# Sparse attention in a two-layer trunk: small reciprocals, and weight remainders by an accumulating DMA

## The chip, the cores and the metric
One core of a Trainium2 chip runs the whole program. The metric is device microseconds of one execution. TensorE multiplies matrices, VectorE and ScalarE do elementwise work, GpSimd (POOL in the profile) does elementwise work in SBUF and issues DMAs, SyncE (SP) issues DMAs.

## What is computed
The trunk has two layers on 512 tokens of width 1024. Layer 0 mixes tokens by a gated linear recurrence (HGRN), layer 1 by sparse attention; each is followed by a feed-forward block with a convolution. The change touches layer 1 alone:

```python
def dsa_mixer(x, w_in, w_out, rel_bias):        # shortened
    q, k, v, q_idx, k_idx, w_idx = jnp.split(x @ w_in, cuts, axis=-1)
    # 16 query heads and 2 key heads of 64, 8 index heads of 64
    dots = jnp.einsum('bthd,bsd->bths', qib, k_idx)
    scores = jnp.einsum('bths,bth->bts', jax.nn.relu(dots), wb)
    scores = jnp.where(admissible, scores, NEG_BIG)
    _, sel = lax.top_k(scores, top_k)           # top_k = 128
    logits = einsum(q, k[sel]) * 64 ** -0.5 + rel_bias[bucket(q_pos - sel)]
    probs = jax.nn.softmax(jnp.where(valid, logits, NEG_BIG), axis=-1)
    return einsum(probs, v[sel]) @ w_out
```

## The kernel before
Every f32 matrix product is made of three products in a reduced format: each operand is split into a large part and the remainder, and `mm3` adds large by large, large by remainder and remainder by large. `wunit` loads one unit of weights (up to 128x1024) into `wr` and splits it: ScalarE copies the large part `whi`, another engine subtracts it from the raw weights and writes the remainder `wlo`. Each of the tags `wr`, `whi` and `wlo` has three buffers. The list `lo_engine` says who makes the remainder: VectorE, GpSimd, or, where it holds `None`, no engine. In that last form ScalarE writes the negated large part into `wlo`, and a DMA issued by GpSimd reads the raw weights from DRAM once more and adds them to it. The HGRN layer's second half uses that form (19 units); the sparse attention doesn't.

A projection of 128 columns (`proj_T`) is eight calls of `mm3`, 24 matmuls, for one unit of weights. In the sparse attention there are fifteen: the index key and index weights (72 columns), four blocks of index queries, K, V, and eight blocks of queries, in that order (`head_in`, then `rest_in`). The remainders of the first two units are made by VectorE, those of the next eleven by GpSimd, those of the last two query blocks by VectorE.

The order on TensorE is the order in which the program emits its matmuls: a main generator is woven with side generators, by estimated TensorE times written in the code. Beside `head_in` run the norm (`norm_chain`, whose line 253 copies the reciprocal row scales on ScalarE) and `setup` (four loads of shifted bias rows from the DRAM tensor Z by SyncE, lines 728 to 734, copied into `bias` by ScalarE). Beside `rest_in` run `dots` (index scores on VectorE, line 764), `top` (sixteen rounds of finding and striking out the eight largest, lines 778 and 780, then a mask, line 783) and `attend`. On all the other engines a planner orders the instructions at build time, by emission order and by the costs and ready times that it reckons with; at run time each engine keeps that order.

`attend` goes through 16 units of half the tokens and two heads each. `scores` multiplies queries and keys, adds the mask as a product with the identity (line 863) and the bias on VectorE (line 873, which also takes a minimum), and makes the exponentials with their sums on ScalarE (line 892). The reciprocals of the sums stand in `rs`, each repeated over 64 columns, since TensorE transposes them together with the probabilities (lines 914 and 917). `mixv` copies the transposed block to SBUF on ScalarE (`px`, line 918), multiplies by the values (lines 925 and 928) and scales on VectorE (line 932). `stack` writes large parts on ScalarE (lines 675 and 676) and remainders on VectorE or GpSimd (677 and 678); `scaled` evacuates a product through ScalarE and GpSimd (699 and 700). `kw_weights` transposes the index weights on TensorE (line 717) and needs the row scales.

Of the kernel before, what the change touches and what calls it, by code (L numbers as in the profile page):

```python
# [17 lines left out]
P = 128  # L18
# [30 lines left out]
def trunk(ctx: ExitStack, tc: tile.TileContext, xT, vecs, convs, hgrn_w_in, hgrn_w_out, dsa_w_in, dsa_w_out,  # L49
          rel_bias, ffn_w_up, ffn_w_down, c_masks, c_onehot, out, dbg=None, stop=99):  # L50
    nc = tc.nc
# [85 lines left out]
    lo_engine = [nc.vector]  # L137
# [49 lines left out]
    def add_side(gen, rate=1.0):  # L187
        side.append([gen, rate, 0.0])

    def step(e):  # L190
        c = next(e[0], None)
        if c is None:
            side.remove(e)
        else:
            e[2] -= c

    def weave(gen):
        for c in gen:
            for e in list(side):
                e[2] += c * e[1]  # L200
                while e in side and e[2] > 0:
                    step(e)
# [458 lines left out]
    with ExitStack() as sx:  # L661
# [26 lines left out]
        with ExitStack() as sy:  # L688
# [33 lines left out]
            def setup():  # L722

                yield 7.0
                nc.vector.tensor_copy(identb, ident)
                nc.gpsimd.memset(vf, 0.0)
                for h in range(0, AH, 4):
                    nc.scalar.activation(bias[:, h:h + 4, :256], far[:, h:h + 4, None].to_broadcast([P, 4, 256]),
                                         AF.Copy, scale=-1.0)

                    back = ix.tile([P, 4, 256], F32, name="back", bufs=2)
                    nc.sync.dma_start(back, bass.AP(tensor=Z.tensor, offset=Z.offset + h * BAND,
                                                    ap=[[1, P], [BAND, 4], [1, 256]]))
                    nc.scalar.activation(bias[:, h:h + 4, 256:], back[:, :, ::-1], AF.Copy)
                    yield 3.0

            def head_in():
                pk = yield from proj_T(w_in, O_KI, 72)
                for b in range(4):
                    o = yield from proj_T(w_in, O_QI + b * P,  # L740
                                          hook=({7: lambda: kw_evac(pk)}, {2: kw_weights}, None, None)[b])
                    lo_engine[0] = nc.gpsimd
                    stack(4 + b, o, nc.vector)

            def dots():
# [57 lines left out]
            def rest_in():  # L803
                pk = yield from proj_T(w_in, O_K)
                pv = yield from proj_T(w_in, O_V, hook={3: lambda: k_out(pk)})
                for b in range(KB):
                    lo_engine[0] = nc.vector if b >= 6 else nc.gpsimd
                    o = yield from proj_T(w_in, b * P, hook={3: lambda: kw.append(scaled(pv)), 7: v_out}
                                          if b == 0 else None)
                    tmp = scaled(o, P, -0.125)  # L810
                    stack(b, tmp, nc.gpsimd)
                    done.add(f"q{b}")
                done.add("q8")

            add_side(norm_chain())
            add_side(setup())
            weave(head_in())
            add_side(dots(), 1.0)
            rest = rest_in()
            for c in rest:  # L820
                weave([c])
# [16 lines left out]
        def scores(u):  # L838


            hf, b = u
# [45 lines left out]
            sm = at.tile([P, 2, 2], F32, name="sm", bufs=4)  # L887
            rs = at.tile([P, 2, 2, 64], F32, name="rs", bufs=4)
            for e in range(2):
                for j, t in enumerate(tiles):  # L890
                    l = L[e][j][:, :(t + 1) * P]
                    nc.scalar.activation(l, l, AF.Exp, bias=mn[e][:, j:j + 1], scale=-1.0, accum_out=sm[:, j, e:e + 1])
            nc.vector.reciprocal(rs, sm[:, :, :, None].to_broadcast([P, 2, 2, 64]))
            probs[u] = L, rs
            if {"sel3", "q8"} <= done:
                later = [c for f, c in units[units.index(u) + 1:] if f]
# [144 lines left out]
```

## Time and profile before

| | |
|---|---|
| median of 3 runs | 1279.28 us (1279.26 to 1279.95) |
| profiled execution | 1283.4 us |
| its span, first to last instruction | 1281.6 us |
| mean granted TensorE clock | 0.991 |
| TensorE busy | 1256.1 us, 98% |
| VectorE busy | 820.5 us, 64% |
| ScalarE busy | 597.3 us, 47% |
| GpSimd busy | 155.8 us, 12% |

The profile is of one execution; the runs are timed without it. Times of rows are microseconds from the span's start unless marked ns. Matmuls are pipelined, so a busy TensorE is not one at its peak. A granted clock of 1.00 is 2.4 GHz; the other level is 1.2 GHz, and a stretch between 0.5 and 1.00 had both. The sparse attention up to its output product takes the stretch from 669 to 860 us.

### The profile page before, as it was taken

What the parts mean: (1) busy time and instruction counts of PE and PEld (TensorE: products, weight loads), DVE (VectorE), ACT (ScalarE), POOL (GpSimd) and SP (SyncE); (2) the same over time, 40 slices, a digit from 0 to 9 for tenths busy, and PEclk for the clock granted to TensorE, in tenths of its full rate; (3) what the DMA queues carried; (4) which work ended last, traced back from release to release, by engine and by line L of the source; (5) the groups of instructions that cost most, each with busy time, mean ns of one, the idle gap of its engine ahead of it and who ended that gap; (6) DMA issues with size and microseconds to landing.
All of it is one profiled execution on the core that took longest, in us unless ns stands there. A gap on an engine that the chain in (4) does not pass through costs nothing.

```text
span 1281.6 us, 15660 instructions
## 1 busy us (share of the span) xinstructions
PE 1256.1 (98%) x6054; PEld 1050.0 (82%) x6054; DVE 820.5 (64%) x1279; ACT 597.3 (47%) x991; POOL 155.8 (12%) x130
## 2 busy tenths in 40 slices
PE   8999999999999999999999998999999999999997
PEld 7788888888888888888877777898888888888886
DVE  7755777756777777732434999945677777762331
ACT  5446565454544444422336657854444444441330
POOL 3023223110000000000004574210000000000000
PEclk9999999999999999999999989999999999999998
DMA  6339777223333333323244220102333333333222
GB/s 198 116 80 152 131 131 132 67 66 99 97 93 92 97 99 99 99 99 99 76 114 134 65 66 17 34 1 84 97 99 99 98 93 92 95 99 99 91 75 66
DMA packets 190857, 119.84 MB, mean 94 GB/s; under 512 B 5136, under 2 KB 180160, under 8 KB 190784
## 3 DMA queue, kind: packets, MB, share of 16 engines
q1 hardware_dynamic: 170320, 108.31, 28.5%
q0 software_dynamic: 19760, 9.96, 6.4%
q8 instruction: 47, 0.77, 0.2%
q10 hardware_dynamic: 704, 0.58, 0.2%
q14 instruction: 26, 0.21, 0.1%
HBM read 116.72 MB, written 2.12 MB: 93 GB/s over the span
## 4 chain that ended last, share of the span: by engine, by line
PE 90%; DVE 6%; ACT 1%; issue 1%; DMA 0%; POOL 0%; POOLq 0%; DVEq 0%; ACTq 0%
PE pj L169 17%; PE pj L170 17%; PE pj L171 17%; PE px L169 9%; PE px L171 9%; PE px L170 9%; PE pav L925 2%; PE pl L556 1%; PE po L602 1%; DVE scs L764 1%; PE pl L866 1%; PE pt L914 1%; PE pn L169 1%; PE pn L171 1%; PE pn L170 1%
## 5 line engine op out<-in xcount | busy, mean ns | idle before, releaser
L169 PE MATMUL pj<-x,whi 128*128 128x512 f32 (+1 forms) x1016 | 404.9, 398 | 0.0
L170 PE MATMUL pj<-x,whi 128*128 128x512 f32 (+1 forms) x1016 | 398.2, 392 | 0.0
L171 PE MATMUL pj<-x,wlo 128*128 128x512 f32 (+1 forms) x1016 | 398.1, 392 | 0.0
L143 ACT ACTIVATE whi<-wr 128x1024 fp32r<-128x1024 f32 (+1 forms) x175 | 181.9, 1040 | 253.6 <-PE px L170 152.3
L144 DVE TENSOR_TENSOR wlo<-wr,whi 128x1024 fp32r<-128x1024 f32 (+2 forms) x165 | 202.0, 1225 | 152.4 <-ACT whi L143 150.3
L171 PEld LDWEIGHTS pj<-x,wlo 128*128 128x128 f32 (+1 forms) x1016 | 191.8, 189 | 41.2
L169 PEld LDWEIGHTS pj<-x,whi 128*128 128x128 f32 (+1 forms) x1016 | 192.1, 189 | 39.6 <-issue 1.6
L170 PEld LDWEIGHTS pj<-x,whi 128*128 128x128 f32 (+1 forms) x1016 | 192.0, 189 | 38.9 <-issue 1.0
L169 PE MATMUL px<-ah,whi 128*128 128x512 f32 (+1 forms) x332 | 128.5, 387 | 0.0
L171 PE MATMUL px<-ah,wlo 128*128 128x512 f32 (+1 forms) x332 | 127.5, 384 | 0.0
L170 PE MATMUL px<-al,whi 128*128 128x512 f32 (+1 forms) x332 | 126.3, 381 | 0.0
L348 DVE TENSOR_TENSOR ub<-pj,rstd_r 128x512 f32<-128x512 f32 x88 | 60.6, 688 | 82.8 <-PE pj L171 77.9
L143 ACT ACTIVATE ah<-c 128x512 fp32r<-128x512 f32 x44 | 27.8, 631 | 115.9 <-DVE c L360 115.9
L171 PEld LDWEIGHTS px<-ah,wlo 128*128 128x128 f32 x332 | 62.3, 188 | 13.5
L170 PEld LDWEIGHTS px<-al,whi 128*128 128x128 f32 x332 | 62.4, 188 | 12.7
L351 ACT ACTIVATE c<-ub,convc 128x512 f32<-128x512 f32 x88 | 71.2, 809 | 2.4 <-DVE ub L348 1.6
L169 PEld LDWEIGHTS px<-ah,whi 128*128 128x128 f32 x332 | 62.5, 188 | 11.4
L353 DVE SCALAR_TENSOR_TENSOR c<-ub,convc,c 128x512 f32<-128x512 f32 x88 | 66.1, 752 | 3.0
L352 DVE SCALAR_TENSOR_TENSOR c<-ub,convc,c 128x512 f32<-128x512 f32 x88 | 65.6, 746 | 0.0
L358 ACT ACTIVATE c<-c 128x512 f32<-128x512 f32 x44 | 27.8, 632 | 80.5 <-DVE c L353 80.4
L522 DVE TENSOR_TENSOR qk<-qk,ftree 128x512 f32<-128x512 f32 x56 | 39.6, 709 | 18.9 <-PE pl L560 7.1
L144 DVE TENSOR_TENSOR al<-c,ah 128x512 fp32r<-128x512 f32 x44 | 30.5, 692 | 29.3 <-ACT ah L143 29.3
(226 smaller groups left out, 1768.8 us busy)
## 6 DMA issues: line engine op xcount, KB each, us to landing
wr<-in_ffn_w_up_dram SPq DMA_DIRECT2D x88, 512.0 KB, 3.8
wr<-in_ffn_w_down_dram SPq DMA_DIRECT2D x41, 512.0 KB, 3.7
wr<-in_hgrn_w_in_dram SPq DMA_DIRECT2D x30, 512.0 KB, 4.2
wlo<-in_hgrn_w_in_dram POOLq DMA_DIRECT2D x19, 512.0 KB, 7.7
wr<-in_dsa_w_in_dram SPq DMA_DIRECT2D x14, 512.0 KB, 3.7
wr<-in_hgrn_w_out_dram SPq DMA_DIRECT2D x8, 512.0 KB, 3.7
wr<-in_dsa_w_out_dram SPq DMA_DIRECT2D x8, 512.0 KB, 3.8
back<-Z SPq DMA_DIRECT2D x4, 512.0 KB, 5.1
```

Of the source, the lines that this page charges most:

```text
L143: nc.scalar.activation(dst_h, src, AF.Copy)
L144: lo.tensor_tensor(dst_l, src, dst_h.bitcast(F32), op=ALU.subtract)
L169: nc.tensor.matmul(o, ah, bh, start=start, stop=False)
L170: nc.tensor.matmul(o, ah, bl, start=False, stop=False)
L171: nc.tensor.matmul(o, al, bh, start=False, stop=stop)
L348: nc.vector.tensor_tensor(u[:, 2:], o, rows(), op=ALU.mult)
L351: nc.scalar.activation(c, u[:, 2:], AF.Identity, scale=cc[2], bias=cc[3])
L352: nc.vector.scalar_tensor_tensor(c, u[:, 1:T + 1], cc[1], c, op0=ALU.mult, op1=ALU.add)
L353: nc.vector.scalar_tensor_tensor(c, u[:, 0:T], cc[0], c, op0=ALU.mult, op1=ALU.add)
L358: nc.scalar.activation(g, g, AF.Silu)
L522: nc.vector.tensor_tensor(turned(m), turned(m), factors(ft, m), op=ALU.mult)
L925: nc.tensor.matmul(o[:, :256], vf[:, s, kv, c], px[:, e, s * 256:s * 256 + 256], start=e == 0 and s == 0, stop=False)
```

## The change
It has two parts. In `scores`, VectorE takes the reciprocals of the four sums in place, and a second instruction copies them to the 256 columns of `rs`; before, one reciprocal read the broadcast sums and wrote 256 columns. And `lo_engine` is set to `None` ahead of `head_in` and not again until the projections are done, so that all fifteen units of the input projections have their remainders made as in the HGRN layer: a negated copy on ScalarE, and an accumulating DMA of the raw weights. The units of the output projection keep VectorE.

```diff
 def head_in():
     ...
-                    lo_engine[0] = nc.gpsimd
                     stack(4 + b, o, nc.vector)
 def rest_in():
     ...
                 for b in range(KB):
-                    lo_engine[0] = nc.vector if b >= 6 else nc.gpsimd
                     o = yield from proj_T(w_in, b * P, hook={3: lambda: kw.append(scaled(pv)), 7: v_out}
                                           if b == 0 else None)
     ...
             add_side(norm_chain())
             add_side(setup())
+            lo_engine[0] = None
             weave(head_in())
 def scores(u):
     ...
-            nc.vector.reciprocal(rs, sm[:, :, :, None].to_broadcast([P, 2, 2, 64]))
+            nc.vector.reciprocal(sm, sm)
+            nc.vector.tensor_copy(rs, sm[:, :, :, None].to_broadcast([P, 2, 2, 64]))
```

## Rows read from the trace of the kernel before

**Rows 1.** The page's chain that ended last, by engine.
```profile
PE 90%; DVE 6%; ACT 1%; issue 1%; DMA 0%; POOL 0%; POOLq 0%; DVEq 0%; ACTq 0%
```
**Rows 2.** Stages: length, busy us of PE, PEld, DVE, ACT, POOL, clock, DMA.
```profile
669.00:677.00 8.00, 7.11 (x30) 4.03 (x29) 5.30 (x6) 7.19 (x9) 3.75 (x2) 1.00 1.00 270
677.00:700.00 23.00, 23.00 (x107) 18.98 (x106) 9.03 (x15) 12.73 (x17) 10.56 (x5) 1.00 0.44 122
700.00:724.00 24.00, 23.89 (x116) 20.23 (x116) 21.90 (x41) 15.71 (x30) 10.18 (x7) 1.00 0.20 55
724.00:736.00 12.00, 9.79 (x39) 7.67 (x38) 11.55 (x36) 7.01 (x10) 9.42 (x8) 0.86 0.33 89
...
743.00:754.00 11.00, 8.05 (x33) 6.57 (x31) 11.00 (x31) 6.09 (x14) 7.45 (x6) 0.69 0.16 48
...
775.00:812.00 37.00, 32.59 (x223) 29.09 (x222) 35.07 (x102) 29.42 (x91) 12.61 (x11) 1.00 0.10 30
```
**Rows 3.** TensorE's timeline: start, us, instruction, and the idle time before it.
```profile
746.48 0.59 PE L863 MATMUL pl<-sel,identb 128*128 128x256 bf16 x2 [2.95 <-DVE sel L783]
...
783.04 0.70 PE L925 MATMUL pav<-px,vf 128*128 128x256 f32 x2 [1.22 <-ACT px L918]
...
787.21 0.70 PE L925 MATMUL pav<-px,vf 128*128 128x256 f32 x2 [0.54 <-ACT px L918]
...
802.96 0.33 PE L917 MATMUL pt<-ident,rs 128*128 128x128 f32 x1 [0.67 <-DVE rs L893]
```
**Rows 4.** VectorE: reciprocals and a broadcast copy (min, median, max ns), two score accumulations.
```profile
L893 DVE RECIPROCAL rs<-sm x16: 1726/1752/1754, 753.0 to 847.1; 128x256 f32<-128x256 f32 x16
...
L402 DVE RECIPROCAL lbr<-lb_e x1: 203/203/203, 5.7 to 5.7; 128x8 f32<-128x8 f32 x1
...
L116 DVE CAST pairs<-wr x3: 286/286/286, 28.7 to 29.1; 128x256 uint8<-128x256 f32 x3
...
712.77 0.60 DVE L764 SCALAR_TENSOR_TENSOR scs<-relu,wN,scs 128x384 f32<-128x384 f32 x1
...
713.64 2.42 DVE L764 SCALAR_TENSOR_TENSOR scs<-relu,wN,scs 128x384 f32<-128x384 f32 x1
```
**Rows 5.** The remainders made by GpSimd and VectorE, 655 to 812 us.
```profile
L144 POOL TENSOR_TENSOR wlo<-wr,whi x11: 2347/2402/2486, 671.0 to 743.9; 128x1024 fp32r<-128x1024 f32 x11
L144 DVE TENSOR_TENSOR wlo<-wr,whi x7: 759/1215/2264, 655.1 to 803.8; 128x1024 fp32r<-128x1024 f32 x5, 128x768 fp32r<-128x768 f32 x1, 128x576 fp32r<-128x576 f32 x1
```
**Rows 6.** The HGRN layer's accumulating DMAs and negated copies.
```profile
L160 POOL DMA_DIRECT2D wlo<-in_hgrn_w_in_dram x19: 1546/1560/1745, 82.6 to 226.9; - x19
...
DMA to landing us min/median/max: 7.1/7.7/8.7
...
L158 ACT ACTIVATE wlo<-wr x19: 1040/1043/1108, 81.2 to 225.5; 128x1024 fp32r<-128x1024 f32 x19
```
**Rows 7.** DMA: GpSimd's queue, 122 to 230 us (packets, MB, share); bias loads.
```profile
q0 software_dynamic: 13563, 6.84, 52.8%
...
back<-Z SPq DMA_DIRECT2D x4, 512.0 KB, 5.1
```
**Rows 8.** ScalarE's timeline, in the HGRN layer and among the index projections.
```profile
124.65 1.06 ACT L159 ACTIVATE whi<-wr 128x1024 fp32r<-128x1024 f32 x1 [1.21 <-PE pj L170]
125.62 1.04 ACT L158 ACTIVATE wlo<-wr 128x1024 fp32r<-128x1024 f32 x1
...
688.74 1.06 ACT L143 ACTIVATE whi<-wr 128x1024 fp32r<-128x1024 f32 x1 [2.33 <-issue]
689.83 0.59 ACT L675 ACTIVATE qh<-pj 64x512 fp32r<-64x512 f32 x1
...
694.18 1.06 ACT L143 ACTIVATE whi<-wr 128x1024 fp32r<-128x1024 f32 x1 [3.15 <-issue]
```
**Rows 9.** ScalarE's timeline: the last bias copy and the row scales.
```profile
681.54 1.06 ACT L734 ACTIVATE bias<-back 128x1024 f32<-128x1024 f32 x1 [0.37 <-DMA back<-Z]
682.50 0.58 ACT L253 ACTIVATE rstd_r<-pr 128x512 f32<-128x512 f32 x1
```

## The prediction, made before the change was run
> **What bounds the kernel now.** I began with the chain that ended last: nine tenths of it is TensorE, 6% VectorE [rows 1]. So only TensorE's waits, and stretches in which its clock is down, can be won; a busy microsecond saved on another engine counts only if it ends such a wait. The table by stage says where these are in the sparse-attention layer [rows 2]: 0.89 us before 677 us, nothing from 677 to 700, 0.11 to 724, then 12 - 9.79 = 2.21 us around 730, 11 - 8.05 = 2.95 us after 743, and 37 - 32.59 = 4.41 us from 775 to 812; in the intervals left out of the rows it waits for nothing. In all 10.6 us. The granted clock is 0.86 in the stretch around 730 and 0.69 in the one after 743, which is 12 x 0.14 = 1.7 and 11 x 0.31 = 3.4 us of full-speed clock more, of which some 0.4 lie inside the wait itself. Everything that this change can win lies in these 15 us or so, 1.2% of the span.
>
> The waits by themselves say who is late [rows 3]. At 746.48 TensorE waits 2.95 us for the first selection mask, the last link of a chain of VectorE rounds. After 775 it waits for ScalarE's copies of the transposed probabilities (1.22, 0.54) and for the reciprocals themselves (0.67). VectorE is busy 35.07 of those 37 us [rows 2].
>
> **The reciprocals.** Sixteen of them, 1752 ns each, 28.0 us of VectorE [rows 4]. In their place stand sixteen reciprocals of four sums and sixteen copies to 256 columns. The trace has near relatives of both: a reciprocal of eight columns took 203 ns, a broadcast copy of f32 to 128x256 took 286 [rows 4]. So 0.49 for 1.75 us, 1.26 us less per unit and 20 us less VectorE in all. About two of the sixteen run before 775, where TensorE waits for nothing of theirs. The rest lie in the last stretch and after it. Between 775 and 812 a unit's exponentials cannot start before VectorE has added the bias, and that stands behind the reciprocal of the unit before; the copies on ScalarE stand behind the exponentials. With 1.26 us gone from a unit, waits of 0.54 and 0.67 have no cause left. The 1.22 is different: ScalarE is then behind with the last query block's evacuation, which waits for GpSimd. Bounds: nothing (ScalarE, 29.42 us busy of 37, takes VectorE's place) and all 4.41. I take what is left without the first wait, 4.41 - 1.22 = 3.2, rounded down to **3.0 us won**, since the queues stay in order.
>
> **The second parts: what is removed.** Eleven subtractions on GpSimd, 2402 ns each (26.4 us), and four on VectorE, two for the first index blocks and two for the last query blocks, in a group that runs from 0.76 to 2.26 us [rows 5]. Beside the GpSimd ones VectorE is slow: the score accumulation of 384 columns took 0.60 us just before, and 2.42 with a subtraction running [rows 4]. The difference, 1.82 us, lies ahead of the mask for which TensorE waits. Other GpSimd work stays and can hit the same instructions, and part of the accumulation is paced by TensorE's dot products. Bounds: nothing, and the whole wait of 2.95 us. I take **1.8 us won**. The two subtractions of the last query blocks free VectorE by some 3.5 us more before 775 (2.26 and a median 1.2), in a stretch without a TensorE wait; it makes the 3.0 above safer and is not counted again.
>
> **What is added.** Fifteen negated copies on ScalarE, 1043 ns each, 15.6 us, and fifteen accumulating DMAs, fourteen of 512 KB, each 1560 ns of GpSimd [rows 6]: 23.4 us on GpSimd for the 26.4 taken off. ScalarE has room (15.71 of the 24 us from 700 on [rows 2]), but the second part now comes late: a DMA lands 7.1 to 8.7 us after its issue, 7.7 in the middle [rows 6], where the subtraction took 2.4. The projection begins with its first weight block's second part, so TensorE waits if it has not landed.
>
> The weights have three buffers. A unit's buffer is free when the unit three before it ends, and then two units of 694.18 - 688.74 = 5.44 us run, 10.9 us [rows 8]. In the earlier stage that has this form, ScalarE made the large part first and the negated one behind it, 2.01 us from start to end [rows 8]; with 7.7 us that is 9.7 (9.1 to 10.7): in time. In the attention stage the stacking copies, 0.59 each [rows 8], may go between the two, since they become ready together with the freed buffer: 10.9 us (10.3 to 11.9). So it is a matter of tenths for the units between 677 and 700, and none where dot products or scores stand between the units.
>
> The tight place is 669 to 677 us: the DMA engines' share is 1.00 there, with the bias loads of 512 KB each in flight [rows 2, 7]. An accumulating DMA is heavy: 52.8% of 108 us for 6.84 MB, or 13 DMAs, is 4.4 us of all sixteen engines [rows 7]. Two or three of them fall on this burst. Whatever they push back stands in order on ScalarE: the bias copies wait for their loads (0.37 us already), and behind them stands the copy of the row scales [rows 9], without which the index projection isn't evacuated, whose transposes TensorE has in its order at 685 us. Bounds for all these stalls: nothing, and two DMAs, 8.8 us. I take **1.5 us lost**, nearer to the stage that the form is known from, where the landings fit.
>
> The Trainium skill (DMA: Bandwidth & Descriptors, section Queues, rings and completion order) says that each DMA engine takes turns between the queues that have work. By that rule the bias loads would get every second turn only and the burst would end up to two transfers later; what that comes to is the first rival. No row of this trace shows the turns themselves: in the burst one queue is at work. The Trainium skill (SBUF — State Buffer, section SBUF: two separate sides) also warns that VectorE's f32 copy in SBUF keeps GpSimd from writing descriptors for as long as it runs; that is no more than one copy's length per DMA, and the issues beside a busy VectorE in this trace, 1546 to 1745 ns, show little of it.
>
> **The sum.** The profiled execution has a span of 1281.6 us and a time of 1283.4; the median of the runs shown is 1279.28, 4.1 below that. -3.0 - 1.8 + 1.5 = -3.3 us: span 1278.3, and from the median **1276.0 us**.
>
> **The rivals.**
> First, late landings decide (23%). The accumulating DMAs and the bias loads share the engines from 667 to 685 us, the bias copies hold up the row scales on ScalarE, and TensorE waits at 685 us and for the weights of the second and third index block. Slipping by one DMA costs 4.4 us, and after a wait of 2.2 us the clock was down by 1.7 us' worth [rows 2]: 6.1 - 4.8 = +1.3, 1280.6 us. By two: 8.8 + 1.7 - 4.8 = +5.7, 1285.0. It ends slower by over 0.2% from 4.8 + 2.6 = 7.4 us of stalls. For it speaks the share of 1.00; against it that ScalarE's order there may change, with the row scales ahead of the bias copies.
> Second, VectorE is freed and TensorE's waits stay (27%): ScalarE is next in the last stretch, and the mask is paced by the dot products. Half of the gain, 2.4, less 1.5: -0.9, 1278.4 us.
> Third, the wait at 743 us gets so short that the clock stays up (15%). Waits of 1.22 us after 775 left it at 1.00, those of 2.21 and 2.95 us went with 0.86 and 0.69 [rows 2, 3]. That gives 3.0 more: -6.3, 1273.0 us.
> The forecast itself has 35%.
>
> **The numbers.** 0.2% is 2.6 us, about what a measurement of this kernel can tell from no change. Faster by over that: nearly all of the third, most of the forecast's own range (1273.5 to 1278), little of the others: 46%. Slower: the larger half of the first and the worst of the second: 20%. Within: 34%. Eight times in ten the time lies between 1270 us (the third with the whole last stretch) and 1284 us (two DMAs late with the gains as summed).
>
> **What would show it.** Right: the reciprocal and its copy at about 0.5 us together; no wait over 0.3 us on probabilities after 785; the wait for the first mask under 1.5 us; accumulating DMAs landing 7 to 9 us after issue, and no wait over 0.5 us of TensorE between 669 and 700. Wrong: bias loads landing more than 8 us after issue and a TensorE wait at the transposes of the index weights; waits for second parts in back-to-back units; ScalarE as releaser of every wait after 775. The order on ScalarE, VectorE and GpSimd is planned anew when the program is built; a plan that puts the negated copies behind the exponentials or the DMAs behind GpSimd's stacking would make the prediction wrong by several microseconds.

## The result, and the profile after

Slower: 1288.21 us (median of 4 runs, 1284.86 to 1289.04) against 1279.37 for the kernel before, ratio 1.0058, interval 1.0046 to 1.007. The forecast was 1276.0, the range 1270 to 1284. The profiled execution after took 1284.86 us, with a span of 1283.1.

TensorE's waits in the sparse-attention layer, 660 to 810 us of the kernel after: engine, line, what it waited for, us in total, times, longest.

```profile
PE pav L925 <- ACT px L918: 5.1, 2, 4.0
PE pj L171 <- ACT bias L734: 4.5, 1, 4.5
PE pj L171 <- DMA wlo<-in_dsa_w_in_dram: 2.1, 1, 2.1
PE pr L252 <- POOL rstd_c L248: 1.5, 1, 1.5
PE pl L862 <- DVE sel L782: 0.7, 1, 0.7
```

The first mask, for which TensorE waited 2.95 us [rows 3], now costs 0.7. In its place stand 4.5 us and 2.1 us for second parts and 4.0 us for the first probabilities; a wait of 2.21 us in the kernel before, at 727 us, is gone:

```profile
727.16 0.66 PE L800 MATMUL pt<-ident,tmp 128*128 128x128 f32 x4 [2.21 <-POOL tmp L700]
```

The wait of 4.5 us names a bias copy; the weights' second part is an input of L171 too, and in the repeat of this kernel below the wait goes by its DMA.

The table by stage of the kernel after (columns as in [rows 2]):

```profile
669.00:677.00 8.00, 7.05 (x29) 4.58 (x27) 2.53 (x5) 5.52 (x7) 2.08 (x2) 1.00 0.91 223
677.00:700.00 23.00, 17.92 (x70) 14.39 (x71) 5.44 (x11) 13.43 (x17) 5.23 (x4) 0.85 1.00 185
...
724.00:736.00 12.00, 11.85 (x55) 9.57 (x54) 12.00 (x31) 10.14 (x17) 8.24 (x7) 1.00 0.76 117
736.00:743.00 7.00, 4.86 (x15) 3.52 (x14) 7.00 (x26) 3.69 (x5) 6.07 (x6) 0.76 1.32 242
743.00:754.00 11.00, 10.26 (x52) 8.59 (x51) 11.00 (x38) 7.70 (x16) 6.76 (x6) 1.00 0.89 139
775.00:812.00 37.00, 31.86 (x216) 29.35 (x215) 24.71 (x97) 28.83 (x87) 16.80 (x11) 0.95 0.14 44
```

From 677 to 700 us TensorE was busy all 23 us before [rows 2]; now 17.92, and at a clock of 0.85, so 23 x 0.15 = 3.5 us more are gone. After 743 the clock stays at 1.00 (before 0.69). In the last stretch VectorE is busy 24.71 us for 35.07, and TensorE still does less.

Where the time went is read by setting each TensorE instruction's start in one trace against the same instruction's start in the other; their order is the same in both. The work ahead of the layer, which the change doesn't touch, ended 3.4 us earlier in this execution. From the start of the first index-key product to the start of the last product of probabilities and values, called **the stage** from here on, it is 190.7 us before and 195.9 after: +5.2.

| stretch (us, before) | forecast | after's lead or lag at its ends | change |
|---|---|---|---|
| index units, to 686 | +1.5 | -3.4 to +4.7 | +8.1 |
| to 737 | in that | +4.7 to +5.0 | +0.3 |
| first mask, to 752 | -1.8 | +5.0 to +0.4 | -4.6 |
| first probabilities, to 783 | 0 | +0.4 to +5.8 | +5.4 |
| rest of the last stretch and to the end | -3.0 | +5.8 to +1.8 | -4.0 |
| stage | -3.3 | | +5.2 |

Both gains came, larger than forecast. Two losses took them back.

The +0.3 to 737 us hides an exchange. Up to 735 us TensorE made up 3.7 us, since the wait of 2.21 us for GpSimd's row scaling of the values is gone. From there to 738 us it lost 4.0 again, by this wait for a second part and a lower clock behind it (0.66 from 738 to 743 us):

```profile
738.61 0.50 PE L171 MATMUL pj<-x,wlo 128*128 128x512 f32 x1 [2.15 <-DMA wlo<-in_dsa_w_in_dram]
```

**The first loss.** ScalarE and GpSimd of the kernel after, by time:

```profile
672.55 1.06 ACT L734 ACTIVATE bias<-back 128x1024 f32<-128x1024 f32 x1 [2.48 <-DMA back<-Z]
673.52 1.04 ACT L158 ACTIVATE wlo<-wr 128x1024 fp32r<-128x1024 f32 x1
...
674.91 1.55 POOL L160 DMA_DIRECT2D wlo<-in_dsa_w_in_dram  x1 [7.23 <-ACT wlo L158]
675.82 1.70 POOL L248 TENSOR_TENSOR rstd_c<-ms,half 128x4 f32<-128x4 f32 x1
677.75 1.59 POOL L160 DMA_DIRECT2D wlo<-in_dsa_w_in_dram  x1 [0.23 <-issue]
```

The negated copy of the second index block stands behind a bias copy that waits 2.48 us for its load; the DMA goes out at 674.91, ahead of the `rstd_c` for which TensorE then waits 1.5 us. The two DMAs issued there, from the view of line L160 between 674 and 679 us:

```profile
L160 POOL DMA_DIRECT2D wlo<-in_dsa_w_in_dram x2: 1546/1570/1594, 674.9 to 677.8; - x2
...
DMA to landing us min/median/max: 10.2/11.2/12.2
```

674.9 + 10.2 = 685.1, when TensorE goes on.

**The second loss.** VectorE, GpSimd and ScalarE of the kernel after, by time:

```profile
776.05 0.69 DVE L782 TENSOR_SCALAR sel<-scs 128x384 bf16<-128x384 f32 x2
776.65 3.49 DVE L144 TENSOR_TENSOR wlo<-wr,whi 128x1024 fp32r<-128x1024 f32 x3
...
776.17 5.10 POOL L678 TENSOR_TENSOR ql<-tmp,ql 64x512 fp32r<-64x512 f32 x1
781.35 2.27 POOL L835 TENSOR_TENSOR scs<-bias,sel 128x512 f32<-128x512 f32 x2
783.57 1.27 POOL L700 TENSOR_TENSOR tmp<-tmp,rstd_r 128x512 f32<-128x512 f32 x1
...
781.30 0.60 ACT L699 ACTIVATE tmp<-pj 128x512 f32<-128x512 f32 x1 [4.00 <-POOL ql L678]
781.80 1.08 ACT L918 ACTIVATE px<-pt 128x512 f32<-128x512 f32 x2
```

VectorE ends the selection at 776.65, 9.6 us earlier than before (786.3, by the row below), and takes three subtractions for the output projection in a row. GpSimd's stacking, 1.29 us elsewhere, lasts 5.10 beside them. ScalarE's next copy overwrites what GpSimd is reading, so it waits 4.00 us, and the probabilities stand behind it. The selection's last masks in the kernel before:

```profile
785.62 0.69 DVE L783 TENSOR_SCALAR sel<-scs 128x384 bf16<-128x384 f32 x2
```

The reciprocals cost what the prediction said, 178 + 294 ns, 0.47 us for 1.75. From the views of lines L892 and L893 after:

```profile
L892 DVE RECIPROCAL sm<-sm x16: 152/178/180, 754.9 to 848.9; 128x4 f32<-128x4 f32 x16
...
L893 DVE COPY rs<-sm x16: 279/294/681, 755.5 to 849.1; 128x256 f32<-128x256 f32 x16
```

### The profile page after: what moved, and what is told of

Its sections match the earlier page's. It is cut to its first block, busy times and chain, and to the rows that moved or that the text cites. A ratio compares the mean times of both kernels' runs of the same rounds, so it can differ in the third digit from the quotient of the medians.

```text
span 1283.1 us, 15718 instructions
## 1 busy us (share of the span) xinstructions
PE 1255.0 (98%) x6054; PEld 1048.3 (82%) x6054; DVE 791.6 (62%) x1291; ACT 610.8 (48%) x1006; POOL 156.6 (12%) x134
## 5 line engine op out<-in xcount | busy, mean ns | idle before, releaser
L171 PE MATMUL pj<-x,wlo 128*128 128x512 f32 (+1 forms) x1016 | 398.1, 392 | 6.8 <-ACT bias L734 4.5
L144 DVE TENSOR_TENSOR wlo<-wr,whi 128x1024 fp32r<-128x1024 f32 (+1 forms) x161 | 195.3, 1214 | 145.2 <-ACT whi L143 143.1
L143 ACT ACTIVATE whi<-wr 128x1024 fp32r<-128x1024 f32 (+1 forms) x160 | 166.6, 1041 | 233.5 <-PE px L170 147.3
L171 PEld LDWEIGHTS pj<-x,wlo 128*128 128x128 f32 (+1 forms) x1016 | 191.4, 188 | 49.0 <-ACT bias L734 4.9
L171 PE MATMUL px<-ah,wlo 128*128 128x512 f32 (+1 forms) x332 | 127.5, 384 | 0.0
L171 PEld LDWEIGHTS px<-ah,wlo 128*128 128x128 f32 x332 | 62.3, 188 | 13.5
L160 POOL DMA_DIRECT2D wlo<-in_dsa_w_in_dram x15 | 23.5, 1566 | 382.6 <-ACT wlo L158 382.3
L159 ACT ACTIVATE whi<-wr 128x1024 fp32r<-128x1024 f32 (+1 forms) x34 | 35.5, 1045 | 51.7 <-PE pj L170 31.4
```

Of the source, the lines that this page charges most:

```text
L143: nc.scalar.activation(dst_h, src, AF.Copy)
L144: lo.tensor_tensor(dst_l, src, dst_h.bitcast(F32), op=ALU.subtract)
L159: nc.scalar.activation(hi[:, :nk * n], raw[:, :nk * n], AF.Copy)
L160: nc.gpsimd.dma_start(lo[:, :nk * n].rearrange("p (k n) -> p k n", k=nk), src.rearrange("(k p) n -> p k n", p=P), accum_op=ALU.add)
L171: nc.tensor.matmul(o, al, bh, start=False, stop=stop)
```

## The experiments

Medians of the runs against the kernel before on the same chip; the stage is from each kernel's trace. Runs of one kernel lie up to 7 us apart (12 runs of e3: 1277.4 to 1284.3; 23 of before: 1278.8 to 1283.9). TensorE's clock ahead of the stage is not the same in every trace either: from 7 to 13 us it was 0.72 in the trace of before and 1.00 in that of after. The stage's length leaves that out. By the medians the kernel after loses 8.8 us, 6.5 in its repeat, where the stage loses 5.2 and 5.6; where the rest lies was not shown.

| kernel | us | ratio to before, interval | stage, us |
|---|---|---|---|
| before | 1279.4 to 1280.1 | | 190.7 |
| after, once more (e0) | 1286.58 | 1.0047, 1.0035 to 1.0059 | 196.3 |
| e1 reciprocals only | 1281.61 | 1.0007, 0.9998 to 1.0016 | 191.8 |
| e2 weights only | 1285.71 | 1.0041, 1.0027 to 1.0054 | 194.9 |
| e3 DMA from the keys on | 1279.81 | 0.9999, 0.9988 to 1.001 | 188.4 |
| e4 prefetched units too | 1285.93 | 1.0049, 1.0033 to 1.0066 | 194.9 |
| e5 = e3, last query on VectorE | 1278.58 | 0.9992, 0.9983 to 1.0001 | 190.0 |
| e6 bias code put off | 1284.47 | 1.0036, 1.0025 to 1.0047 | 194.9 |
| e7 = e1, last query on VectorE | 1279.08 | 1.0, 0.999 to 1.0009 | 189.2 |
| e8 spread | 1279.24 | 0.9992, 0.9983 to 1.0001 | 188.8 |
| e9 one bias load | 1286.25 | 1.0041, 1.0028 to 1.0054 | 195.1 |
| e10 = e3, odd queries on GpSimd | 1281.50 | 1.0007, 0.9997 to 1.0017 | 190.7 |
| e11 spread, two scalings on VectorE | 1274.68 | 0.9963, 0.9951 to 0.9976 | 186.0 |
| e12 = e6 and e9 | 1282.56 | 1.0017, 1.0008 to 1.0026 | 192.0 |
| e13 other spread | 1277.63 | 0.9986, 0.9977 to 0.9995 | 187.6 |
| e14 = e11, long reciprocals | 1278.65 | 0.9994, 0.9985 to 1.0003 | 187.9 |
| e15 = e11, no DMA | 1278.48 | 0.9988, 0.9979 to 0.9997 | 188.1 |

### Is the loss the stage's own? The kernel after again

> The changed kernel once more, nothing altered. In its first trace the attention stage, from the first product of the index keys to the last product of probabilities and values, takes 195.9 us against 190.7 before (+5.2), while the work ahead of it ended 3.4 us earlier than before, with no change there. Theory A, the loss is the stage's own: the stage takes 195 to 197 us again, with waits of about 4.5 us at the second index block's second part and about 4 us for the first probabilities, wherever the work ahead of it ends; the time is 1285 to 1289 us. Rival B, the loss is a matter of when the clock happens to rise and fall: the stage comes out anywhere between 190 and 200 us and the two long waits are not both there.

Theory A. The waits are the same, each within 0.5 us (1.6, 4.8, 2.6, 0.7, 4.1), the stage is +5.6, and the changes in the table above are +8.3, +0.7, -4.7, +5.4 and -4.0 here, though the work ahead ended only 2.1 us early. The release that was put down to a bias copy now reads so:

```profile
PE pj L171 <- DMA wlo<-in_dsa_w_in_dram: 7.4, 2, 4.8
```

### Each part alone

The kernel before with the two lines of the reciprocals:

```diff
-            nc.vector.reciprocal(rs, sm[:, :, :, None].to_broadcast([P, 2, 2, 64]))
+            nc.vector.reciprocal(sm, sm)
+            nc.vector.tensor_copy(rs, sm[:, :, :, None].to_broadcast([P, 2, 2, 64]))
```

> The reciprocals changed, the weights' second parts as before. Theory A: the reciprocals won what they were said to, 3 to 4 us between 787 and 807 us, and the loss is the weights' alone: 1275 to 1277 us, the stage 187 to 188 us. Against it stands that VectorE, freed, takes up subtractions for the output projection's weights earlier (in this program two of them stand in a row, in the changed kernel three): if GpSimd stands still beside them, 1 to 3 us of it are given back, 1277 to 1279 us. Rival C, the new copies to 256 columns are what holds up GpSimd and ScalarE: 1280 us or more, and GpSimd's stacking instructions of 1.29 us last 2 us or more wherever a copy runs.

1281.61 us: no gain in the time, outside theory A and its allowance. Rival C's time (1280 or more) was met, but not its mark: GpSimd's stacking beside the first copy to 256 columns took 1.33 us (it was the copy that took 1.35 for 0.29). The gain is in the trace all the same, 3.3 us from 787 us on, but 5.6 us are lost just ahead of it. Its waits and GpSimd's timeline:

```profile
PE pav L926 <- ACT px L919: 5.6, 1, 5.6
PE pl L863 <- DVE sel L783: 4.5, 1, 4.5
PE pt L800 <- POOL tmp L700: 2.3, 1, 2.3
...
776.90 2.01 POOL L836 TENSOR_TENSOR scs<-bias,sel 128x512 f32<-128x512 f32 x1 [3.12 <-DVE sel L783]
778.87 1.26 POOL L700 TENSOR_TENSOR tmp<-tmp,rstd_r 128x512 f32<-128x512 f32 x1
780.09 2.13 POOL L836 TENSOR_TENSOR scs<-bias,sel 128x512 f32<-128x512 f32 x1
```

The order on VectorE and GpSimd is another one. With short reciprocals the selection ends before the attention's first units, and a mask now stands ahead of the last query block's row scaling on GpSimd: it waits 3.12 us for the selection, then the scaling comes, and ScalarE with the probabilities behind it. So the reciprocals alone bring such a loss, without an accumulating DMA, though what stands in front here is a mask and in the kernel after the subtractions and the stacking beside them.

The kernel after with the old reciprocal line:

> All fifteen units with the accumulating DMA, the reciprocals as before. From the two traces: 8.1 us lost up to the transposes of the index weights, 0.3 around 735 us, 4.5 won at the first mask, nothing in the last stretch, since without the short reciprocals VectorE does not take three subtractions in a row there. Theory A: +3.9 us, 1283 us, the stage about 194.6 us, no GpSimd stacking over 2.5 us around 776 us. Rival C, the long wait for the first probabilities comes from the accumulating DMAs and not from VectorE's order: it is there again, and the time is 1288 us or more.

Theory A: stage +4.1 against +3.9 worked out, though the time, 1285.7, lies above its 1283. With e1's +1.0 that makes 5.1, nearly the whole of the change (+5.2). The waits for second parts (7.8 us in two) and for `rstd_c` (1.6) are those of the kernel after; none for probabilities is over 1.8. And with the long reciprocals nothing is won from 787 to 812 us: 0.5 us are lost there, and 0.5 are won in e14 below, where each of the fifteen traces with the short ones wins 2.9 to 3.3.

### DMA only where the units have room

The index units as before; `None` from the keys on (short reciprocals; shortened):

```diff
-            lo_engine[0] = None
             weave(head_in())
             add_side(dots(), 1.0)
+            lo_engine[0] = None
             rest = rest_in()
```

with `lo_engine[0] = nc.gpsimd` back in `head_in`.

> The changed kernel, but the five units of the index projections keep their subtractions on VectorE and GpSimd; the accumulating DMA serves only the ten units from the keys on. Theory A, the burst of bias loads between 667 and 690 us is what makes the accumulating DMAs late: the 8.1 us lost there are gone, the subtractions beside the first scores are partly back (1 to 2 us lost at the first mask), and the wait of 4 us for the first probabilities stays: stage 188 to 190 us, time 1278 to 1281 us. Rival D, the accumulating DMA is late in any unit of this stage: waits of 2 us or more at the second parts of the keys, values and queries, and the time stays at 1285 us or more.

Theory A on the whole: stage 188.4, and not even the loss allowed for at the first mask, 743 to 754 us being without a wait. The index units are where the 8 us were lost. Two waits are left, 2.8 us at 729 for a second part, where the three DMAs issued from 722 to 732 us landed after 8.6 to 10.4 us, and 6.0 for the first probabilities. At the second of them:

```profile
770.07 5.42 DVE L144 TENSOR_TENSOR wlo<-wr,whi 128x1024 fp32r<-128x1024 f32 x3
...
770.29 4.11 POOL L836 TENSOR_TENSOR scs<-bias,sel 128x512 f32<-128x512 f32 x2 [0.43 <-DVE sel L783]
774.36 2.25 POOL L700 TENSOR_TENSOR tmp<-tmp,rstd_r 128x512 f32<-128x512 f32 x1
...
776.64 0.63 ACT L675 ACTIVATE qh<-tmp 64x512 fp32r<-64x512 f32 x1 [5.18 <-POOL tmp L700]
```

Three subtractions take 5.42 us here and 3.49 in the kernel after; two masks take 4.11 us here and 2.27 there. Side by side each slows the other.

### What makes the first probabilities late

The kernel after, with the accumulating DMA for the two output units fetched ahead (`lo_engine[0] = None` around them):

> The changed kernel, with the first two units of the output projection, which are fetched ahead during the attention, also given the negated copy on ScalarE and the accumulating DMA. Then VectorE has one subtraction, not three, in a row ahead of the first units' bias additions at 776 us. Theory A, the three subtractions (3.5 us) hold up GpSimd's last stacking (5.1 us in place of 1.29), and through it ScalarE and the first probabilities: the stacking lasts 1.3 to 2.5 us, the wait of about 4 us falls to 2 us or less, the stage is 193 to 194.5 us, the time 1.5 to 3 us less than the changed kernel's, 1284 us. Rival C, the wait is ScalarE's own (its exponentials stand behind the last query block whatever GpSimd does): the wait stays near 4 us and the two further copies of 1.06 us on ScalarE make it longer.

Between the two: GpSimd's stacking is back to 1.27 us, but two waits of 1.4 and 4.0 stay. One subtraction is left on VectorE, and GpSimd still makes two masks (3.13 us) ahead of the last query block's scaling. So the three subtractions are not the cause by themselves; what stands in front of that scaling counts too.

The last query block's scaling and stacking on VectorE, in e3 and in e1 (shortened):

```diff
-                    tmp = scaled(o, P, -0.125)
-                    stack(b, tmp, nc.gpsimd)
+                    eng = nc.vector if b == 7 else nc.gpsimd
+                    tmp = scaled(o, P, -0.125, eng)
+                    stack(b, tmp, eng)
```

> As the kernel with the accumulating DMA from the keys on, where the first probabilities waited 5.99 us, but the row scaling and the stacking of the last query block are VectorE's and not GpSimd's, so that the masks of GpSimd no longer stand in front of them. The three subtractions still stand in a row on VectorE, and the scaling now stands behind them. Theory A, GpSimd's standstill beside VectorE is most of that wait: it falls to about 3 us or less, the time to 1276 or 1277 us. Rival E, VectorE's queue takes GpSimd's place, since ScalarE waits for the scaling of the last query block in either case: the wait stays at 5 us or more and the time at 1279 to 1280 us.

> The reciprocals changed and the weights as before, with the row scaling and the stacking of the last query block on VectorE; in this program GpSimd makes its masks after all of that. In the kernel with the reciprocals alone the first probabilities waited 5.59 us, GpSimd working through masks (2.0 and 2.1 us) between the last block's steps. Theory A: with GpSimd out of that chain the wait is 2 us or less and the gain of the reciprocals shows: 1276 to 1278 us. Rival E, the wait moves to VectorE's queue: it stays over 4 us, and the time is 1280 to 1282 us as with the reciprocals alone.

In e5 nearer to rival E: ScalarE waits 4.65 us for VectorE's scaling, which stands behind the three subtractions; the wait falls only from 6.0 to 4.7. In e7, with one subtraction ahead, it falls from 5.6 to 3.1, and the stage is 2.6 us shorter than with the reciprocals alone, short of theory A's mark.

### What makes the second parts late

The kernel after, bias code put off (`yield 24.0` for 7.0 in `setup`):

> The changed kernel, with the bias loads and bias copies put off by about 17 us of products, so that they no longer share the DMA engines and ScalarE with the first accumulating DMAs. Theory A, the burst is what makes the second index block's second part late: the waits of 1.6 and 4.5 to 4.8 us before 690 us fall below 2 us together and the granted clock from 677 to 700 us stays above 0.95; the landing of the accumulating DMAs in that stretch falls from 10 to 12 us to 7 to 8. Stage about 189 to 191 us, time 1280 to 1283 us. Rival D, back-to-back projections cannot hide this DMA at all: a wait of 3 us or more remains at the second index block though the bias loads are gone.

Neither as written: the loads still went out at 667 us, only ScalarE's order changed. The negated copies came in time, the two DMAs issued from 668 to 679 us landed after 10.4 and 11.7 us, and 5.7 us of waits (1.1, 2.0, 2.6) remain before 700 us, with the clock at 0.96.

> The changed kernel with one bias load in place of four: all four bias copies read the first block's values, so 1.5 MB less pass through the DMA engines around 670 us and three bias copies wait for nothing (three quarters of the bias near the diagonal are therefore other values). The run with the bias code put off did not answer this, as its loads were issued at 667 us all the same. Theory A, the bias loads make the first accumulating DMAs late: the waits before 700 us fall from 6.1 us to 2 us or less, the granted clock there stays above 0.95, stage 188 to 190 us, time 1279 to 1282 us. Theory F, five index units back to back need 4.4 us of all sixteen engines for each accumulating DMA and some 1.9 us for each raw load, 6.3 us in every 5.4 us of products, with or without the bias: waits of 3 us or more remain before 700 us, and the time is 1282 to 1285 us.

Theory A's marks are missed: 4.4 us are left at the same place with 1.5 MB less on the DMA engines, over theory F's mark of 3. But the loads are a part of it. The two accumulating DMAs issued from 678 to 682 us landed after 6.9 and 8.7 us (10.2 and 12.2 in the kernel after), the wait for `rstd_c` is gone, and TensorE loses 5.1 us up to 700 us where it lost 8.1. The stage is hardly shorter since later waits grew (6.0 us for the first probabilities against 4.0, 2.8 at 736 against 2.1). What is left stands on ScalarE, where the negated copy is behind two bias copies, and so the DMA goes out 1.5 us later in the stage:

```profile
675.57 2.01 ACT L732 ACTIVATE bias<-back 128x1024 f32<-128x1024 f32 x2 [3.00 <-DMA back<-Z]
677.49 1.04 ACT L158 ACTIVATE wlo<-wr 128x1024 fp32r<-128x1024 f32 x1
```

Its large part, from the same raw weights, was copied at 668.48, 9.0 us earlier (7.5 in the kernel after: 665.98 and 673.52). Both at once:

> The changed kernel with both halves of the bias work out of the way of the first accumulating DMAs: one load in place of four (the other three blocks read the first one's values), and the bias code put off, so that the negated copies of the first index blocks stand ahead of the bias copies on ScalarE. Each alone left the waits: with one load the negated copy of the second index block still stood behind bias copies on ScalarE (7 us after its raw weights had landed); with the code put off the copies came in time, but the DMAs took 10 to 12 us beside the bias loads. Theory A, the two together are the cause: the waits before 700 us fall to 1.5 us or less in all, stage 188 to 190 us, time 1279 to 1281 us. Theory F, accumulating DMAs and raw loads for units back to back are themselves too much for the DMA engines: a wait of 2 us or more remains before 700 us, stage 192 us or more.

2.7 us of waits remain before 700 us, 2.08 of them at 692 us for a second part whose DMA went out at 686.25 and took an ordinary 7.75 us; stage 192.0, and 4.0 us lost up to 700 us. So of the 8.1 us some 4 are the bias work's: 3.0 go with its loads alone (e9), 1.2 with its copies alone (e6, which loses 6.9). Part of what is left is theory F's: in units back to back an accumulating DMA is late by itself. The DMA engines' share there is 0.98 even now, which is no limit by itself: from 736 to 743 us of the kernel after it was 1.32. That the engines' time, and not the late issue behind the stacking copies, holds these units up was not shown.

### Versions built from this

Odd query units back on GpSimd, in e3 (shortened):

```diff
+                    lo_engine[0] = nc.gpsimd if b % 2 else None
                     o = yield from proj_T(w_in, b * P, hook=...
```

> The kernel with the accumulating DMA from the keys on, but the odd query units keep the subtraction on GpSimd; the rest is unchanged, so also the last query block on GpSimd and the three subtractions on VectorE. Theory F, the DMA engines cannot bring one accumulating DMA and one raw load for each of several units back to back: with every second one gone the wait of 2.80 us at 729 us falls below 1 us and the landings of the others from 9 to 10 us to 7; the wait of 6 us for the first probabilities stays; stage 185 to 187 us, time 1276 to 1278 us. Rival H, a subtraction on GpSimd at 722 us delays the values' row scaling and the first query block as the kernel with the reciprocals alone showed (2.34 us at 723): a wait of 2 us or more near 723 to 730 us stays and the time does not change.

By its marks rival H: 2.2 us at 722 us for the values' scaling, and still 2.7 at 731. But no weight subtraction on GpSimd stood ahead of that scaling: GpSimd had been idle for 1.77 us, waiting for ScalarE's copy. Then also the prefetched units by DMA, and the last query block wholly on VectorE, scaled straight from PSUM:

> A kernel built from what the runs so far say, with the short reciprocals: the index units, and every second query unit, keep their subtractions on VectorE and GpSimd; the accumulating DMA serves keys, values, the even query blocks and the two output units fetched ahead; the last query block is scaled and stacked by VectorE alone, straight from PSUM, so that neither ScalarE nor GpSimd has work of it. Theory A (an accumulating DMA for every one of several units back to back is more than the DMA engines can bring in time, and ScalarE standing behind the last query block is what makes the first probabilities late): the wait of 2.8 to 3.6 us at 729 us is under 1 us, the wait of 4 to 6 us for the first probabilities under 2 us, the stage 183 to 186 us against 190.7 before, the time 1273 to 1276 us. Rival G, the first probabilities are late because the selection rounds end there on VectorE, whoever stacks the last block: a wait of 3 us or more stays around 775 us, and the time is 1277 to 1279 us.

Theory A only in part, 188.8 us. The two places that held it up, VectorE and ScalarE by time:

```profile
773.28 0.69 DVE L816 SCALAR_TENSOR_TENSOR tmp<-pj,rstd_r 128x512 f32<-128x512 f32 x1 [3.29 <-POOL ql L682]
...
777.86 0.40 ACT L902 ACTIVATE L<-L,mn 128x128 f32<-128x128 f32 x1 [5.05 <-DVE mn L883]
```

There is one `tmp` buffer, still read by GpSimd for the block before; and the bias additions of the first units stand behind VectorE's stacking. Both mended, with the values' scaling on VectorE too (the kernel after against the new one, shortened):

```diff
+                    if b == 7:
+                        tmp = iy.tile([P, T], F32, name="tmp7")
+                        nc.vector.scalar_tensor_tensor(tmp, o, -0.125, rows(), op0=ALU.mult, op1=ALU.mult)
+                    else:
+                        tmp = scaled(o, P, -0.125)
-                    tmp = scaled(o, P, -0.125)
                     stack(b, tmp, nc.gpsimd)
```

> As the kernel with the work spread (odd queries on GpSimd, two output units by DMA), with two changes from its trace. The values' row scaling is VectorE's, straight from PSUM, since TensorE waited 2.22 us at 722 us for GpSimd's. And the last query block is scaled by VectorE into a buffer of its own, so that it does not wait 3.29 us for GpSimd to stack the block before, and is stacked by ScalarE and GpSimd, behind the first two masks, where VectorE's bias additions of the first units do not stand behind it. Theory A (what stands in order ahead of the first probabilities on ScalarE and VectorE makes them late): no wait over 1.5 us at 722 us and none over 2 us around 775 us; stage 182 to 185 us, time 1272 to 1276 us. Rival G, the attention starts as soon as the last projection allows and the selection of the last tiles is not ahead of it by then: 3 us or more of waits stay between 770 and 782 us, stage 187 to 189 us, time 1278 to 1280 us.

1274.68 us, 0.9963 of before: the first version that is clearly faster. Its waits, 660 to 812 us:

```profile
PE pav L936 <- ACT px L929: 2.3, 2, 2.0
PE pj L171 <- DMA wlo<-in_dsa_w_in_dram: 2.1, 1, 2.1
PE pt L800 <- DVE tmp L805: 2.1, 1, 2.1
PE pq L240 <- DVE sqa L215: 0.9, 1, 0.9
PE pl L873 <- DVE sel L783: 0.4, 1, 0.4
```

The first probabilities wait 2.0 us for 4.0, as theory A has it; the stage is 1 us outside its range, since the wait at 722 us only changed its name (VectorE for GpSimd). The other spread, with odd and even changed about from the third query on:

> As the last but one, but keys, values and the first two query blocks have the accumulating DMA, the third, fifth and seventh GpSimd's subtraction, and the values' scaling stays on GpSimd. Theory A: no wait at 722 us (GpSimd has no subtraction ahead of the values' scaling), the wait of 2.8 us for the second query block's second part at 729 us is there again, none over 2 us around 775 us: stage 182 to 185 us, time 1273 to 1276 us. Rival G: 3 us or more of waits between 770 and 782 us, stage 187 us or more, time 1278 us or more.

No wait at 722 or 729, but one of 6.3 us for the first mask, half the clock after it: what TensorE saved it met at the mask, which VectorE's rounds set. The mask came 76.9 us after the stage's start, and it comes 74.9 to 77.2 us after it in every kernel whose index units are as before. 187.6 us.

Last, each part of the change taken out of e11:

> The fastest kernel so far (1274.7 us; values and last query block scaled by VectorE, accumulating DMAs spread) with the reciprocals of 256 columns put back, 1.75 us for 0.49. It says what the first part of the change is worth once nothing of the last query block stands ahead of the first probabilities. Theory A, the prediction's term of 3 us holds there: the waits on probabilities and reciprocals between 785 and 805 us (0.3 to 0.7 us each) are back, stage 188 to 190 us against 186.0, time 1277 to 1279 us. Rival I, the term is only the early end of the selection rounds and is hidden either way: within 1 us of 1274.7 us.

> The same fastest kernel with all second parts made by subtractions as before, no accumulating DMA in this stage: what the second part of the change is worth where it is spread out. Theory A, it takes GpSimd's subtractions from beside the score accumulations and so ends the wait for the first mask: without it that wait (4.5 us in the kernel with the reciprocals alone) is back, with a lower clock after it, stage 188 to 190 us, time 1277 to 1279 us. Rival I, the two moved scalings do all of it: within 1 us of 1274.7 us.

Both as theory A on time (0.9994 and 0.9988 against 0.9963), and 1.9 and 2.1 us longer in the stage: 187.9 is just under the range of 188 to 190, 188.1 at its lower end. The waits that came back, first of e14, then of e15:

```profile
PE pav L935 <- ACT px L928: 6.6, 5, 2.0
```

```profile
PE pl L872 <- DVE sel L783: 3.7, 1, 3.7
```

So with the new waits out of the way the reciprocals are worth 2 to 4 us (1.9 by the stage, 0.0031 x 1280 = 4.0 by the ratios), and the spread DMAs 2 to 3 (2.1, and 0.0025 x 1280 = 3.2). From 775 us on e14 loses 3.6 us against e11; the stage shows less since it waits 1.6 us less for a second part at 733 us. In e15 the mask has only a part in the loss: up to 752 us 0.9 of the 2.1 us are lost, for its wait stands where e11 waits 2.1 us for a DMA. The other 1.2 are lost from 775 us on, and why was not shown.

## Why the prediction was wrong

**The reciprocals, 3.0 us.** The mechanism was right: 0.47 us for 1.75, the waits of 0.54 and 0.67 gone, -4.0 us from 783 us on, 2.9 to 3.3 us from 787 to 812 us in every trace with the short ones, and 2 to 4 us in e14. But the sum took VectorE's freed time before 775 us as "safer and not counted again". That is a step that failed. The order is planned anew: the selection ended 9.6 us earlier, beside the last query block's evacuation, and masks and subtractions stepped in front of it on GpSimd and VectorE. That costs 5.4 us up to 783 us, with 4.0 of wait. The reciprocals alone lose 5.6 us up to 787 us in e1, with another order in front. The prediction named the risk of a new plan in its last sentence, with other orders (negated copies behind exponentials, DMAs behind stacking) and "several microseconds", but gave it no chance and no place in the sum. Its signs say the same: a wait of 1.19 us on probabilities stands at 789 us, where none over 0.3 was to be, and ScalarE releases every wait of TensorE after 775, which was named as a sign of being wrong.

**The first mask, 1.8 us.** Right in its sign, too small: the wait fell from 2.95 to 0.7 us and the clock stayed at 1.00, -4.6 us. That clock was the third rival (15%), and it happened. The size was luck in part. From the first score accumulation to the end of the first mask VectorE took 43.0 us before and 41.2 after, 1.8 us less, as the term has it. But the accumulations that the prediction read (2.42 us for 0.60) lie 33 us earlier, and little of what they gained, 17.1 to 15.9 us in all, arrives at the mask. Most of what shrank is the mask's own instruction (1.4 us), which ran beside a GpSimd subtraction before and without one after:

```profile
743.93 2.35 POOL L144 TENSOR_TENSOR wlo<-wr,whi 128x1024 fp32r<-128x1024 f32 x1
744.62 1.80 DVE L783 TENSOR_SCALAR sel<-scs 128x256 bf16<-128x256 f32 x1
...
748.98 0.41 DVE L782 TENSOR_SCALAR sel<-scs 128x256 bf16<-128x256 f32 x1
```

The first two rows are of the kernel before, the last of the kernel after. With the subtractions kept the mask took 1.80 us in e1 and 1.24 in e15, and TensorE waited 4.5 and 3.7 us for it. How long TensorE waits also hangs on when it comes there, as e13 shows.

**The stalls, 1.5 us.** This term was mis-sized: 8.1 + 0.3 us, close to its upper bound of 8.8 and the first rival's two slips. I sized it from the layer the form was known from, where the landings fit. Here the DMAs landed after 10.2 and 12.2 us, not 7.1 to 8.7. The prediction had 2.01 us, and with stacking copies a little more, from the large part to the end of the negated copy; the second index block's negated copy started 7.5 us after its large part, behind bias copies on ScalarE, and the `rstd_c` behind the DMA's issue on GpSimd cost 1.5 us more. The first rival had the right place in the second index block's weights; the row scales on ScalarE and the transposes, which it named too, were not what TensorE waited for. Nor was there "none where dot products or scores stand between the units": the wait of 2.15 us at 738 us is one. Its bounds also took a DMA's packet time (4.4 us of all sixteen engines) for engine time and a share of 1.00 for a full burst; the share of 1.32 from 736 to 743 us of the kernel after says that packet times overlap. Of the signs that were to prove it wrong, the second parts in back-to-back units came; bias loads over 8 us after issue did not (7.3 at most).

The Trainium skill (DMA: Bandwidth & Descriptors, section Queues, rings and completion order) has each engine take turns between queues with work. The trace agrees that both sides pay: beside the accumulating DMAs raw loads of 512 KB took 5.9 and 9.1 us, in the middle 3.8. That the bias loads' share alone decides, e9 refutes: with one load the accumulating DMAs landed earlier (6.9 and 8.7 us), and the wait of 4.4 us stayed, behind the bias copies.

**The range.** Two losses came at once, one on the DMA side and one in VectorE's order; each rival held one mechanism, and the range was made from them singly. Its upper end, two DMAs late, also left out the 1.7 us of clock that the first rival itself counts (1285.0). Nor did the step from the profiled span to the median of the runs (-4.1 us) carry over: the profiled execution of the kernel after was its fastest run, that of before was slower than all of its own.

## What to carry to other kernels

A reserve of time given to one engine is spent by the plan: look at what stands ready for that engine, and what it will then stand in front of on its neighbours. A step that moves to another engine and a DMA has the order of that engine's queue to pass; look there for copies that wait on loads. Price a known form of DMA from the stretch where it will run, with units back to back, not from one with room.

## What the hardware showed

- VectorE's subtractions of two SBUF tensors and GpSimd's tensor operations slow each other: 1.29 to 5.10 us for GpSimd's stacking in the kernel after, 2.27 to 4.11 for two masks in e3, and 3.49 to 5.42 between the same two kernels for VectorE's three subtractions. A mask of 128x256 on VectorE took 1.80 us beside a GpSimd subtraction and 0.41 without. The Trainium skill (SBUF — State Buffer, section SBUF: two separate sides) says that a VectorE instruction with two SBUF inputs contends with a GpSimd instruction that reads SBUF, over a port pair that is locked; the trace agrees for the subtractions.
- An accumulating DMA of 512 KB landed after 7.5 us in the middle in this stage, 12.2 at most; its issue on GpSimd kept to 1542 to 1597 ns beside a busy VectorE.
- After the waits of 4.5 and 2.15 us in the kernel after the granted clock was at half for part of the time (0.55 in the mean from 685 to 692 us, 0.66 from 738 to 743). But not every wait of that length lowers it: after 2.7 us at 748 us in e4, 2.8 at 743 in e2 and 2.7 at 734 in e10 it stayed at 1.00 up to 754 us. What makes the difference was not shown.
